# Four layers, four schedules: other norm heads, and values of two key heads padded apart

## The chip, the cores and the metric

The program runs on one core of a Trainium2 chip. The time is device time in microseconds (us), from one launch of the whole program; lower is better. Engines are TensorE (PE), VectorE (DVE), ScalarE (ACT), GpSimd (POOL) and SyncE (SP, which issues most DMAs).

## The reference: what is computed

One inference step of an encoder of four layers, on 256 prompt tokens and 64 sample tokens (320 together), width 1024, in float32. Layers 0 and 3 mix tokens by latent attention (MLA), layer 1 by stick-breaking attention (SB), layer 2 by sliding-window attention with 16 query heads over 4 key heads and a learned sink for each head (SWA; the "layer with sinks"). Each layer reads

```python
xp = xp + mp                    # mp = mixer(rms_norm(x))
xp = xp + fp                    # fp = conv_ffn(rms_norm(x)), inner width 2816
xp = xp + ple(xp, p_prompt[i], g_ple[i], w_ple_gate[i], w_ple_proj[i])
# ple = sigmoid(rms_norm(x, g) @ w_gate) * (p @ w_proj)
```

with the same for the sample tokens, which also read caches. In the layer with sinks

```python
m = jnp.maximum(jnp.max(s, axis=-1, keepdims=True), sink)
e = jnp.exp(s - m)
p = (e / (jnp.sum(e, axis=-1, keepdims=True) + jnp.exp(sink - m))).astype(v.dtype)
return jnp.einsum('bkgqs,bskd->bqkgd', p, v)
```

Outputs are the final norm of x and the new caches.

## The kernel before

**Layout.** Features lie on the 128 partitions, the 320 tokens on the free axis; x is eight tiles x0 to x7 of 128x320. A float32 product is made of three matmuls (`mm3`, L202 to L204): weight high part by data high part, high by low, low by high. So every operand exists as a pair: ScalarE writes the high part (L160), VectorE subtracts it from the source for the low part (L161); `split` does both.

**Weights.** They stream in 450 chunks of eight 128x128 tiles in the order of use (`fetch`, L168 to L176): SP loads `wraw` (three buffers), ScalarE makes `whi`, and VectorE or GpSimd makes `wlo`. GpSimd does so for every second chunk of the MLA and SB mixers and every third of SWA (`WPOOL`), while `self.wpool` is set; it is set at the mixer's start and cleared at its end. `more_weights` fetches ahead.

**Norms.** The gain is folded into the operand and the factor R = 1/rms is applied behind the projection, at its eviction. `norm_piece(m)` runs as soon as x tile m is final: `h{m}hi` (ScalarE, L305), `h{m}lo` (VectorE, L306), the square `sq` (ScalarE, L314), and the running sum `acc` (L320, on GpSimd but for the last). `norm_sums` sums columns on TensorE with a matrix of ones (L272) and takes the reciprocal root by Newton steps on VectorE (tiles `ncol`, L252 to L258). `spread` puts it on a diagonal (six VectorE operations on tiles called `sq`, L282 and L283), multiplies by minus ones on TensorE (L287), and ScalarE copies the result to `R` (L290).

**A layer.** Mixer; convolutional FFN; then `ple`, the per-layer embedding: its norm's sums and spread, then for each of eight columns a projection `pg`, a tanh, an update of x[m], and the next layer's `norm_piece(m)`. The operands of the FFN's and the embedding's norms are `h0` to `h7` and `ph0` to `ph7`. `prep` loads caches of the next layer and splits and transposes them; it is called ahead of `ple`. For SWA this is `swa_prep` (tiles `K00` to `K11` and `V0`, `V1`; the transposes use the PSUM tag "tp", which has two buffers and is also that of the column sums).

**SWA's core.** For two key-head tiles kt and two pairs of heads, `scores`, softmax (tiles `Pr`, `es`, `su`), `turn` (transposes of the probabilities, tiles `PT`) and `values` follow each other. A tile kt holds two key heads u side by side, 64 columns each. `values` makes, for each u, a PSUM tile with all 128 columns of V and splits only the 64 partitions of u:

```python
s = slice(64 * u, 64 * u + 64)
```

**Order.** A list scheduler with a cost model orders each engine's instructions from the program's order and priorities. Inside `manual_schedule(engines=...)` the named engines keep the program's order; before, that is TensorE alone at the mixers' heads.

## Time and the profile before

| | |
|---|---|
| runs, median of 3 | 1865.1 us (1860.9 to 1867.74) |
| the profiled execution | 1871.49 us, its span 1869.7 us |
| mean granted TensorE clock | 0.983 |
| busy share of the span | PE 96%, DVE 72%, ACT 52%, POOL 30% |
| DMA, mean | 136 GB/s |

The profiled execution is a little above the three runs. Stages by the trace, in us: MLA to 225, FFN 0 to 475, embedding 0 to 510, SB to 660, FFN 1 to 908, embedding 1 to 947, SWA to 1077, FFN 2 to 1320, embedding 2 to 1357, MLA to 1570, FFN 3 to 1820, embedding 3 and the final norm to the end. The granted clock has two levels here, 1.2 and 2.4 GHz (0.5 and 1.0 in the rows).

### The profile page before, as it was taken

The page shows a single profiled execution, that of the slowest core. Times are in us where ns is not written, and L with a number is a line of the kernel's source. Part 1 is how long each engine was busy: PE and PEld are TensorE (multiplying, and loading weights), DVE is VectorE, ACT ScalarE, POOL GpSimd, SP SyncE. Part 2 cuts the span into 40 slices and gives each one's busy share as a digit, 9 for nine tenths or more (in the row PEclk, how much of TensorE's full clock was granted, in tenths as well). Part 3 has the DMA queues.
Part 4 walks back from the last instruction along what each step waited for, and adds up shares of the span by engine and source line. Part 5 has one row for each costly group of instructions (what it writes and reads, how often), then busy time and mean ns, then how long its engine had stood idle before and what let it go on. Part 6 is the DMA issues. An engine that isn't in the chain of part 4 may idle for free.

```text
span 1869.7 us, 32633 instructions
## 1 busy us (share of the span) xinstructions
PE 1798.8 (96%) x12352; PEld 1775.2 (95%) x12352; DVE 1347.4 (72%) x2637; ACT 974.6 (52%) x1849; POOL 565.6 (30%) x834
## 2 busy tenths in 40 slices
PE   7899999999999999999998999999989999999996
PEld 7899999999999999999997899999988999999996
DVE  7876687754779878764578687764788777877546
ACT  5776644433568854433456654343447676434332
POOL 3433333321222234320145043320142334333103
PEclk9999999999999999999997999999999999999998
DMA  5333344444534344444342144444433333444441
GB/s 207 107 112 124 126 138 162 151 150 149 168 128 140 121 133 152 151 148 150 126 157 76 46 143 158 148 154 150 144 124 100 122 129 122 157 147 153 153 147 63
DMA packets 78126, 254.15 MB, mean 136 GB/s; under 512 B 9488, under 2 KB 18192, under 8 KB 77968
## 3 DMA queue, kind: packets, MB, share of 16 engines
q1 hardware_dynamic: 77248, 251.34, 40.5%
q8 instruction: 97, 1.59, 0.4%
q10 hardware_dynamic: 720, 0.71, 0.1%
q14 instruction: 61, 0.50, 0.1%
...
## 4 chain that ended last, share of the span: by engine, by line
PE 41%; DVE 6%; ACT 2%; issue 1%; POOL 1%; DMA 0%; DVEq 0%; SPq 0%; ACTq 0%; POOLq 0%
PE ps L202 13%; PE ps L203 13%; PE ps L204 13%; ACT whi L174 1%; DVE rsh L596 1%; DVE wlo L176 1%; PE ps L272 0%; PE ps L1188 0%; DVE PTl L161 0%; POOL wlo L176 0%; DVE h6lo L306 0%; DVE m L1165 0%; DMA ckt<-ckvT 0%; DVE m L671 0%; ACT Pr L675 0%
## 5 line engine op out<-in xcount | busy, mean ns | idle before, releaser
L174 ACT ACTIVATE whi<-wraw 128x1024 fp32r<-128x1024 f32 x450 | 474.5, 1056 | 443.0 <-PE ps L203 230.4
L176 DVE TENSOR_TENSOR wlo<-wraw,whi 128x1024 fp32r<-128x1024 f32 x381 | 471.1, 1237 | 226.5 <-ACT whi L174 219.5
L176 POOL TENSOR_TENSOR wlo<-wraw,whi 128x1024 fp32r<-128x1024 f32 x69 | 166.9, 2418 | 311.0 <-ACT whi L174 292.8
L384 POOL TENSOR_TENSOR ge<-cv,R 128x256 f32<-128x256 f32 (+1 forms) x176 | 132.8, 774 | 92.8 <-ACT cv L381 92.3
L320 POOL TENSOR_TENSOR acc<-acc,sq 128x320 f32<-128x320 f32 x72 | 77.4, 1075 | 261.6 <-ACT sq L314 259.0
L347 DVE TENSOR_TENSOR x<-x,ps 128x320 f32<-128x320 f32 x128 | 61.1, 482 | 55.7 <-PE ps L204 55.4
L379 DVE SCALAR_TENSOR_TENSOR cv<-G,cols,cv 128x322 f32<-128x322 f32 x176 | 95.9, 552 | 2.4
L388 DVE TENSOR_TENSOR af<-ge,ps 128x320 f32<-128x320 f32 x88 | 42.7, 486 | 67.6 <-POOL ge L384 67.4
L202 PE MATMUL ps<-h0hi,whi 128*128 128x320 f32 x256 | 81.1, 317 | 6.5 <-ACT h0hi L305 6.2
L203 PE MATMUL ps<-h6lo,whi 128*128 128x320 f32 x256 | 79.4, 310 | 3.3 <-DVE h6lo L306 3.3
L202 PE MATMUL ps<-h7hi,whi 128*128 128x320 f32 x256 | 79.2, 311 | 3.3 <-ACT h7hi L305 3.3
L203 PE MATMUL ps<-h0lo,whi 128*128 128x320 f32 x256 | 79.9, 312 | 0.8 <-DVE h0lo L306 0.8
L202 PE MATMUL ps<-h4hi,whi 128*128 128x320 f32 x256 | 79.6, 313 | 1.1 <-ACT h4hi L160 1.1
L203 PE MATMUL ps<-h5lo,whi 128*128 128x320 f32 x256 | 79.4, 310 | 1.2 <-DVE h5lo L161 1.2
L203 PE MATMUL ps<-h7lo,whi 128*128 128x320 f32 x256 | 79.9, 312 | 0.5 <-DVE h7lo L306 0.5
L202 PE MATMUL ps<-h1hi,whi 128*128 128x320 f32 x256 | 79.9, 312 | 0.0
L203 PE MATMUL ps<-h4lo,whi 128*128 128x320 f32 x256 | 79.7, 311 | 0.2 <-DVE h4lo L306 0.2
L203 PE MATMUL ps<-h3lo,whi 128*128 128x320 f32 x256 | 79.9, 312 | 0.0
L203 PE MATMUL ps<-h2lo,whi 128*128 128x320 f32 x256 | 79.9, 312 | 0.0
L203 PE MATMUL ps<-h1lo,whi 128*128 128x320 f32 x256 | 79.8, 312 | 0.0
L204 PE MATMUL ps<-h1hi,wlo 128*128 128x320 f32 x256 | 79.8, 312 | 0.0
L204 PE MATMUL ps<-h0hi,wlo 128*128 128x320 f32 x256 | 79.8, 312 | 0.0
...
## 6 DMA issues: line engine op xcount, KB each, us to landing
wraw<-w SPq DMA_DIRECT2D x450, 512.0 KB, 3.2
...
```

The lines of the kernel that those rows point to most:

```text
L174: nc.scalar.activation(out=hi, in_=raw, func=AF.Copy)
L176: e.tensor_tensor(out=lo, in0=raw, in1=hi.bitcast(F32), op=ALU.subtract)
L202: mm(out, w[0], x[0], start=first, stop=False, **kw)
L203: mm(out, w[0], x[1], start=False, stop=False, **kw)
L204: mm(out, w[1], x[0], start=False, stop=last, **kw)
L320: e.tensor_tensor(out=self.nacc[:, 0:NT], in0=self.nacc[:, 0:NT], in1=sq, op=ALU.add)
L347: self.nc.vector.tensor_tensor(out=self.x[m], in0=self.x[m], in1=p[:, 0:NT], op=ALU.add)
L379: nc.vector.scalar_tensor_tensor(out=cv, in0=gt[:, k:k + GW - 2], scalar=w[k], in1=cv, op0=ALU.mult, op1=ALU.add)
L384: nc.gpsimd.tensor_tensor(out=ge[:, c], in0=cv[:, c.start + o:c.stop + o], in1=R[:, c], op=ALU.mult)
L388: nc.vector.tensor_tensor(out=af, in0=ge, in1=pu[:, 0:NT], op=ALU.mult)
L596: nc.vector.tensor_tensor(out=lo[r, :].bitcast(F32R), in0=qf[r, :], in1=hi, op=ALU.subtract)
```

## The change

1. `norm_piece(7)` squares before it makes the operand; `acc` takes tile 6 on VectorE as well as tile 7.
2. The diagonal is made in `norm_sums` (`diag`), the matmul and R in `spread_mm`.
3. The SB mixer begins with `head`: projection A without its last row tile, then B, with the column sums behind B's second tile; then the last tiles of A and B; then the spread and C. From the last embedding column to the end of this head all four engines keep the program's order, and one chunk more is fetched ahead.
4. `self.wpool` is set by `headed`, behind a mixer's head. Chunks of the heads have their `wlo` on VectorE: VectorE makes 385 instead of 381, GpSimd 65 instead of 69.
5. In `ple` the next layer's `prep` comes behind the embedding's own norm.
6. SWA has no `prep`. Caches are loaded and split, and zeros written, in `keys` and `vals`. Its head is left to the list scheduler. V is padded apart: `V{kt}{u}` holds head u's 64 columns and zeros in the others, so that the products of both heads accumulate in one PSUM tile and three splits over 128 partitions stand for six over 64.
7. In the final norm `fin` carries the sign, and six outputs on VectorE read the spread from PSUM (`negR`); GpSimd does tiles 2 and 6 instead of 2 and 5.

```diff
     def norm_piece(self, m):
+        if m == NK - 1:
+            self.norm_square(m)
+            self.norm_operand(m)
+        else:
+            self.norm_operand(m)
+            self.norm_square(m)
...
-            e = nc.vector if m == NK - 1 or self.wpos == 0 else nc.gpsimd
+            e = nc.vector if m >= NK - 2 or self.wpos == 0 else nc.gpsimd
...
+    def head(self, A, B, C, keep_sum=False):
...
+        for k in range(NK - 1):
+            mm(0, k)
...
+        for k in range(NK - 1):
+            mm(1, k)
+            if k == 1:
+                self.norm_sums(keep_sum)
+        mm(0, NK - 1)
+        mm(1, NK - 1)
+        self.norm_spread()
+        self.proj(*C, h)
...
-            self.nr = self.newton_rsqrt(v)
+            self.nr = self.diag(self.newton_rsqrt(v))
...
         R = self.R
-        after()
+        prep = after()
...
+            if m == NK - 1 and nxt == 1:
+                self.region.enter_context(self.tc.manual_schedule(engines=ALL))
...
     def swa_prep(self, j, pool):
...
+        return None
...
+        self.headed(2)
+        h = self.norm_finish()
...
         def keys(kt):
-            kf, kh = KF[kt], K[kt]
+            kf = T([P, W], "kvf", bufs=2)
+            nc.sync.dma_start(out=kf[:, NT:W], in_=t["wkT"][kt])
...
+            kh = [pair([P, W], f"K{kt}{u}") for u in range(2)]
             for u in range(2):
+                for x in kh[u]:
+                    nc.gpsimd.memset(x[64 * (1 - u):64 * (2 - u), :].bitcast(F32), 0.0)
                 s = slice(64 * u, 64 * u + 64)
-                self.split(kh[u][0][s, 0:NT], kh[u][1][s, 0:NT], kf[s, 0:NT])
+                self.split(kh[u][0][s, :], kh[u][1][s, :], kf[s, :])
...
+            vh = [pair([P, 4, P], f"V{kt}{u}") for u in range(2)]
+            for u in range(2):
+                for x in vh[u]:
+                    nc.gpsimd.memset(x[:, :, 64 * (1 - u):64 * (2 - u)].bitcast(F32), 0.0)
+            pv = four(transposes([vf[:, c:c + P] for c in (0, P, S0 - 64, NT)]))
+            for u in range(2):
+                c = slice(64 * u, 64 * u + 64)
+                self.split(vh[u][0][:, :, c], vh[u][1][:, :, c], pv[:, :, c])
...
-            for u in range(2):
-
-                s = slice(64 * u, 64 * u + 64)
-                p, p2 = self.ps("tp"), self.ps("tp")
-                self.mm3(p[:, 0:256], vv(0), [flat(x[:, 4 + u]) for x in PT], True, True)
+            p, p2 = self.ps("tp"), self.ps("tp")
+            for u in range(2):
+                self.mm3(p[:, 0:256], vv(u, 0), [flat(x[:, 4 + u]) for x in PT], u == 0, u == 1)
...
+            for c, src in ((slice(0, P), p[:, 0:256]), (slice(P, SEQ), p[:, 256:512]), (slice(S0, NT), p2[:, 0:P])):
+                self.split(o[0][:, i2, c], o[1][:, i2, c], two(src))
...
+    def headed(self, kind):
+        self.region.close()
+        self.wpool = WPOOL[kind]
...
+            def after():
...
+                self.norm_start(f"g_mix{self.layers[n + 1]}")
+                return self.prep(self.layers[n + 1])
...
-            if m % 3 == 2:
-                nc.gpsimd.tensor_tensor(out=y, in0=self.fin[m], in1=self.R, op=ALU.mult)
+            if m % 4 == 2:
+                nc.gpsimd.tensor_tensor(out=y, in0=self.fin[m], in1=R, op=ALU.mult)
             else:
-                nc.vector.tensor_tensor(out=y, in0=self.fin[m], in1=self.R, op=ALU.mult)
+                nc.vector.tensor_tensor(out=y, in0=self.fin[m], in1=self.negR, op=ALU.mult)
```

**TensorE at the head of SB, before.** `ps_6362` is the first projection of the mixer, here its last two row tiles; `ps_6393` is the second, whose 24 matmuls stand ahead of the column sums.

```order
L202 MATMUL ps_6362<-h6hi_6306,whi_6273 128x320
L203 MATMUL ps_6362<-h6lo_6307,whi_6273 128x320
L204 MATMUL ps_6362<-h6hi_6306,wlo_6274 128x320
L202 MATMUL ps_6362<-h7hi_6349,whi_6273 128x320
L203 MATMUL ps_6362<-h7lo_6350,whi_6273 128x320
L204 MATMUL ps_6362<-h7hi_6349,wlo_6274 128x320
L202 MATMUL ps_6393<-h0hi_6006,whi_6316 128x320
L203 MATMUL ps_6393<-h0lo_6007,whi_6316 128x320
```

The same place in the change: `ps_6368` is A, `ps_6369` is B, `ps_6404` the column sums.

```order
L205 MATMUL ps_6368<-h6hi_6306,whi_6273 128x320
L206 MATMUL ps_6368<-h6lo_6307,whi_6273 128x320
L207 MATMUL ps_6368<-h6hi_6306,wlo_6274 128x320
L205 MATMUL ps_6369<-h0hi_6006,whi_6318 128x320
L206 MATMUL ps_6369<-h0lo_6007,whi_6318 128x320
L207 MATMUL ps_6369<-h0hi_6006,wlo_6319 128x320
L205 MATMUL ps_6369<-h1hi_6057,whi_6318 128x320
L206 MATMUL ps_6369<-h1lo_6058,whi_6318 128x320
L207 MATMUL ps_6369<-h1hi_6057,wlo_6319 128x320
L275 MATMUL ps_6404<-ones_112,acc_6012 128x2 x3
L205 MATMUL ps_6369<-h2hi_6113,whi_6318 128x320
```

The last row tile of the first projection went from 21 rows behind that projection's start to 43, and the column sums from 48 rows to 27.

**VectorE at the same head, before.** G is the embedding's gate, x_14 and x_15 are x tiles 6 and 7, `ncol` the first Newton tile.

```order
L429 TENSOR_TENSOR G_1286_6344<-ps_6313,R_5941 128x320
L306 SCALAR_TENSOR_TENSOR h6lo_6307<-x_14_99,gains_73,h6hi_6306 128x320
L431 SCALAR_TENSOR_TENSOR G_1286_6344<-G_1286_6344,ps_6220 128x320
L433 TENSOR_TENSOR x_15_101<-x_15_101,G_1286_6344 128x320
L306 SCALAR_TENSOR_TENSOR h7lo_6350<-x_15_101,gains_73,h7hi_6349 128x320
L320 TENSOR_TENSOR acc_6012<-acc_6012,sq_6353 128x320
L176 TENSOR_TENSOR wlo_6454<-wraw_6451,whi_6453 128x1024
L335 TENSOR_SCALAR ncol_6428<-ps_6424 128x3
```

In the change:

```order
L486 TENSOR_TENSOR G_1289_6352<-ps_6315,R_5906 128x320
L325 SCALAR_TENSOR_TENSOR h6lo_6307<-x_14_99,gains_73,h6hi_6306 128x320
L344 TENSOR_TENSOR acc_6012<-acc_6012,sq_6310 128x320
L488 SCALAR_TENSOR_TENSOR G_1289_6352<-G_1289_6352,ps_6220 128x320
L490 TENSOR_TENSOR x_15_101<-x_15_101,G_1289_6352 128x320
L344 TENSOR_TENSOR acc_6012<-acc_6012,sq_6357 128x320
L325 SCALAR_TENSOR_TENSOR h7lo_6361<-x_15_101,gains_73,h7hi_6360 128x320
L179 TENSOR_TENSOR wlo_6395<-wraw_6392,whi_6394 128x1024
L387 TENSOR_SCALAR ncol_6408<-ps_6404 128x3
```

`acc` of tile 6 stands on VectorE, `acc` of tile 7 ahead of `h7lo`, and the chunk whose `wlo` GpSimd made in the head (not seen in the first list) is the `wlo_6395` of the second.

**VectorE ahead of embedding 1's Newton steps, before.** ph7 is the last operand of that norm; K and V are SWA's cache parts from `swa_prep`, and the transposes that V0l and V1l read hold both "tp" buffers.

```order
L306 SCALAR_TENSOR_TENSOR ph7lo_11114<-x_15_101,gains_73,ph7hi_11113 128x320
L320 TENSOR_TENSOR acc_10479<-acc_10479,sq_11117 128x320
L161 TENSOR_TENSOR K00l_11135<-kf_2161_11124,K00h_11134 64x128
L161 TENSOR_TENSOR K01l_11137<-kf_2161_11124,K01h_11136 64x128
L161 TENSOR_TENSOR K10l_11153<-kf_2163_11128,K10h_11152 64x128
L161 TENSOR_TENSOR K11l_11155<-kf_2163_11128,K11h_11154 64x128
L176 TENSOR_TENSOR wlo_11291<-wraw_11288,whi_11290 128x1024
L161 TENSOR_TENSOR V0l_11147<-ps_11148,V0h_11146 128x128
L161 TENSOR_TENSOR V1l_11165<-ps_11166,V1h_11164 128x128
L335 TENSOR_SCALAR ncol_11174<-ps_11170 128x3
```

In the change:

```order
L179 TENSOR_TENSOR wlo_11203<-wraw_11200,whi_11202 128x1024
L344 TENSOR_TENSOR acc_10482<-acc_10482,sq_11116 128x320
L325 SCALAR_TENSOR_TENSOR ph7lo_11120<-x_15_101,gains_73,ph7hi_11119 128x320
L179 TENSOR_TENSOR wlo_11248<-wraw_11245,whi_11247 128x1024
L387 TENSOR_SCALAR ncol_11128<-ps_11124 128x3
```

The six cache splits left this place.

**VectorE in one call of `values`, before** (a stretch of it; u = 0 writes ps_12117 and ps_12118, u = 1 ps_12140 and ps_12141).

```order
L161 TENSOR_TENSOR O0l_12116<-ps_12117,O0h_12115 64x2x128
L1167 TENSOR_SCALAR nb_12514<-m_12513 128x2
L1168 TENSOR_TENSOR es_12515<-cols_111,m_12513 128x2
L161 TENSOR_TENSOR O0l_12116<-ps_12140,O0h_12115 64x2x128
L1215 MEMSET ps_12529 64x4x64
L1165 TENSOR_REDUCE m_12543<-ps_12529 128x4
L161 TENSOR_TENSOR O0l_12116<-ps_12140,O0h_12115 64x2x128
L161 TENSOR_TENSOR O0l_12116<-ps_12141,O0h_12115 64x2x64
```

The whole call in the change:

```order
L164 TENSOR_TENSOR O0l_12105<-ps_12106,O0h_12104 128x2x128
L1220 TENSOR_SCALAR Pr_12239<-Pr_12239,su_12238 128x192
L1244 MEMSET ps_12465 64x2x64
L164 TENSOR_TENSOR O0l_12105<-ps_12107,O0h_12104 128x2x64
L1245 MEMSET ps_12465 64x2x64
L164 TENSOR_TENSOR O0l_12105<-ps_12106,O0h_12104 128x2x128
```

Six splits of 64 partitions became three of 128, and one pair of PSUM tiles serves both heads.

## Rows read from the trace of the kernel before

**Rows 1.** The page: the span, its busy times, and the chain that ended last.

```profile
span 1869.7 us, 32633 instructions
...
PE 1798.8 (96%) x12352; PEld 1775.2 (95%) x12352; DVE 1347.4 (72%) x2637; ACT 974.6 (52%) x1849; POOL 565.6 (30%) x834
...
PE 41%; DVE 6%; ACT 2%; issue 1%; POOL 1%; DMA 0%; DVEq 0%; SPq 0%; ACTq 0%; POOLq 0%
```

**Rows 2.** Windows of 20 us: length, busy time (instructions) by engine, granted clock, DMA share, GB/s.

```profile
480.00:500.00 20.00, 18.84 (x127) 18.34 (x126) 17.40 (x37) 11.87 (x21) 3.51 (x4) 1.00 0.40 132
500.00:520.00 20.00, 17.62 (x107) 16.87 (x107) 14.11 (x19) 8.82 (x14) 5.91 (x6) 0.91 0.46 152
...
900.00:920.00 20.00, 17.75 (x105) 17.36 (x104) 10.22 (x30) 5.56 (x11) 2.09 (x5) 0.85 0.44 139
...
940.00:960.00 20.00, 17.63 (x118) 16.88 (x118) 15.49 (x23) 9.33 (x15) 4.79 (x4) 1.00 0.49 159
...
980.00:1000.00 20.00, 16.23 (x115) 15.57 (x114) 15.53 (x48) 13.21 (x38) 14.85 (x16) 0.98 0.33 113
1000.00:1020.00 20.00, 15.90 (x92) 15.02 (x91) 19.20 (x63) 14.55 (x49) 11.12 (x14) 0.76 0.24 80
1020.00:1040.00 20.00, 17.82 (x106) 16.97 (x106) 13.16 (x51) 11.42 (x42) 0.85 (x2) 0.75 0.00 0
1040.00:1060.00 20.00, 19.64 (x128) 19.39 (x129) 13.21 (x42) 13.12 (x41) 0.35 (x2) 0.83 0.16 55
...
1320.00:1340.00 20.00, 18.77 (x120) 18.52 (x119) 14.11 (x38) 8.76 (x18) 1.37 (x2) 0.91 0.30 99
...
1360.00:1380.00 20.00, 17.81 (x121) 17.33 (x122) 15.17 (x36) 7.41 (x12) 6.81 (x6) 1.00 0.33 110
...
260.00:280.00 20.00, 20.00 (x139) 20.00 (x138) 17.63 (x34) 11.06 (x17) 10.26 (x26) 1.00 0.41 134
```

**Rows 3.** TensorE's waits by releaser: total us, how often, the longest.

```profile
PE ps L287 <- DVE sq L282: 4.5, 3, 2.9
...
PE ps L202 <- ACT Pr L1173: 3.4, 3, 1.9
...
PE ps L202 <- ACT h7hi L305: 3.3, 3, 1.1
PE ps L203 <- DVE h6lo L306: 3.3, 3, 1.1
...
PE ps L272 <- DVE Vl L161: 2.4, 2, 1.2
...
PE ps L272 <- DVE V0l L161: 2.3, 1, 2.3
```

**Rows 4.** Timeline of GpSimd, then VectorE, ahead of the stick-breaking layer.

```profile
509.72 2.39 POOL L176 TENSOR_TENSOR wlo<-wraw,whi 128x1024 fp32r<-128x1024 f32 x1 [1.61 <-ACT whi L174]
...
510.12 2.33 DVE L306 SCALAR_TENSOR_TENSOR h6lo<-x,gains,h6hi 128x320 fp32r<-128x320 f32 x1 [0.33 <-ACT h6hi L305]
...
514.16 0.55 DVE L306 SCALAR_TENSOR_TENSOR h7lo<-x,gains,h7hi 128x320 fp32r<-128x320 f32 x1 [0.63 <-ACT h7hi L305]
```

**Rows 5.** Timeline of VectorE, then TensorE, at layer 1's embedding norm.

```profile
907.92 0.49 DVE L320 TENSOR_TENSOR acc<-acc,sq 128x320 f32<-128x320 f32 x1
...
914.00 1.44 PE L272 MATMUL ps<-ones,acc 128*128 128x2 f32 x6 [2.25 <-DVE V0l L161]
```

**Rows 6.** O0l by shape, ns min/median/max; from the timeline a key split, a clear.

```profile
L161 DVE TENSOR_TENSOR O0l<-ps,O0h x16: 208/398/429, 562.9 to 1043.6; 64x256 fp32r<-64x256 f32 x10, 64x128 fp32r<-64x128 f32 x4, 64x64 fp32r<-64x64 f32 x2
...
974.63 1.06 DVE L161 TENSOR_TENSOR K01l<-kf,K01h 64x320 fp32r<-64x320 f32 x1
...
898.52 0.47 POOL L1077 MEMSET K00h<- 64x448 f32 x1
```

**Rows 7.** Timeline of the last operations: ScalarE, then VectorE.

```profile
1861.97 0.44 ACT L290 ACTIVATE R<-ps 128x320 f32<-128x320 f32 x1 [6.45 <-PE ps L287]
...
1862.85 1.15 DVE L1341 TENSOR_TENSOR h1hi<-h1lo,R 128x320 f32<-128x320 f32 x1
```

More of the change, by code (lines that the diff above doesn't have):

```diff
@@ L276, in spread, with diag @@
     def spread(self, r, pool, tag, bufs=2):
+        return self.spread_mm(self.diag(r), pool, tag, bufs)
+    def diag(self, r):
         nc = self.nc
@@ L284, in spread, with spread_mm @@
                                            op0=ALU.mult, op1=ALU.subtract)
+        return dg
+    def spread_mm(self, dg, pool, tag, bufs=2, sign=-1.0):
+        nc = self.nc
         p = self.ps("tp")
@@ L289, in spread @@
         rb = self.tile(pool, [P, NT], tag, bufs=bufs)
[L290 removed]
+        self.negR = p[:, 0:NT]
+        nc.scalar.activation(out=rb, in_=p[:, 0:NT], func=AF.Copy, scale=sign)
         return rb
@@ L328, in norm_finish @@
         return self.nh
+    def head(self, A, B, C, keep_sum=False):
+        h = self.nh
+        if self.first:
+            w = [[self.take(name, np.arange(k * P, k * P + P), cols) for k in range(NK)] for _, name, cols in (A, B, C)]
+            for k in range(NK):
+                for x, y in zip((A, B, C), w):
+                    self.mm3(x[0], y[k], h[k], k == 0, k == NK - 1)
+            self.norm_sums(keep_sum)
+            return
+        first = [(p, [self.take(name, np.arange(k * P, k * P + P), cols) for k in range(NK)]) for p, name, cols in (A,)]
+        mm = lambda n, k: self.mm3(first[n][0], first[n][1][k], h[k], k == 0, k == NK - 1)
+        for k in range(NK - 1):
+            mm(0, k)
+        p, name, cols = B
+        first.append((p, [self.take(name, np.arange(k * P, k * P + P), cols) for k in range(NK)]))
+        for k in range(NK - 1):
+            mm(1, k)
+            if k == 1:
+                self.norm_sums(keep_sum)
+        mm(0, NK - 1)
+        mm(1, NK - 1)
+        self.norm_spread()
+        self.proj(*C, h)
     def norm_sums(self, keep_sum=False):
@@ L404, in ffn, with ple @@
         return ph, pl
-    def ple(self, i, pool, p_emb, after):
+    def ple(self, i, pool, p_emb, after, nxt):
         nc = self.nc
@@ L427, in ple @@
             self.proj(pg[:, 0:NT], f"pg{i}", cols, h)
+            if m == NK - 1 and nxt == 1:
+                self.more_weights()
             u = self.tile(pool, [P, NT], "G2", bufs=2)
@@ L434, in ple @@
             self.norm_piece(m)
+        return prep
     def rotate(self, pool, src, out, o=DEC):
@@ L901, in project, with weighed @@
                 st[r] = start(r)
-            bd, KT, V = st[r]
-            p = self.ps(tag)
-            self.proj(p[:, 0:NT], f"sq{j}", n * D + np.arange(r * P, r * P + P), h)
+            p, *w = weighed(r, n, tag)
+            self.proj(p, *w, h)
             return lambda: scaled(r, n, p)
+        def weighed(r, n, tag="mm"):
+            return self.ps(tag)[:, 0:NT], f"sq{j}", n * D + np.arange(r * P, r * P + P)
         def scaled(r, n, p):
@@ L1012, in values @@
             O.append(o)
+        ps = [weighed(0, n) for n in range(3)]
+        self.head(*ps)
+        self.headed(1)
         with self.tc.manual_schedule(engines=PE):
-            pq, pk = project(0, 0), project(0, 1)
-            self.norm_sums()
-            pv = project(0, 2)
+            with self.tc.high_priority(AHEAD):
+                scaled(0, 0, ps[0][0])
+                scaled(0, 1, ps[1][0])
             pq1 = project(1, 0, "sc")
-            self.norm_spread()
+            scaled(0, 2, ps[2][0])
             pk1 = project(1, 1, "sc")
-            with self.tc.high_priority(AHEAD):
-                pq()
-                pk()
-            pv()
         self.tc.keep_in_program_order(nc.scalar.preload_act_table_set("natural_log_exp_and_others"))
@@ L1090, in swa, with project @@
         W = NT + WIN
+        self.load_rot(pool)
         T = lambda shape, tag, dt=F32, bufs=1: self.tile(pool, shape, tag, dt, bufs)
         pair = lambda shape, tag, bufs=1: self.pair(pool, shape, tag, bufs)
-        h = self.nh
-        early = {}
-        def product(m, tag="mm"):
-            p = self.ps(tag)
-            self.proj(p[:, 0:NT], f"wq{j}", swa_cols(m), h)
-            return p
-        with self.tc.manual_schedule(engines=PE):
-            for n, m in enumerate((8, 10, 0, 1, 2, 3)):
-                early[m] = product(m, "mm" if n < 3 else "sc")
-                if n == 1:
-                    self.norm_sums()
-                if n == 3:
-                    self.norm_spread()
-        def project(m):
-            p = early.pop(m) if m in early else product(m)
+        self.headed(2)
+        h = self.norm_finish()
+        R = self.R
+        tags = ["sc"] * 3 + ["mm"] * 3
+        def project(m):
+            p = self.ps(tags.pop() if tags else "mm")
+            self.proj(p[:, 0:NT], f"wq{j}", swa_cols(m), h)
             f = T([P, NT], "pf", bufs=2)
-            nc.vector.tensor_tensor(out=f, in0=p[:, 0:NT], in1=self.R, op=ALU.mult)
+            nc.vector.tensor_tensor(out=f, in0=p[:, 0:NT], in1=R, op=ALU.mult)
             return f
@@ L1146, in vals @@
             nc.sync.dma_start(out=t["o_wv"][kt], in_=vf)
-            pv = transposes([vf[:, c:c + P] for c in (0, P, S0 - 64)])[:, 0:3 * P]
-            self.split(vh[0][:, 0:3], vh[1][:, 0:3], pv.rearrange("p (a b) -> p a b", a=3))
+            vh = [pair([P, 4, P], f"V{kt}{u}") for u in range(2)]
[6 more added lines that the diff above has]
+                self.split(vh[u][0][:, :, c], vh[u][1][:, :, c], pv[:, :, c])
+            V.append(vh)
         st = {}
```

70 lines of the change are left out of this document (25 added, 45 removed).

## The prediction

> **What bounds the kernel now.** I read the page first: TensorE is busy for 96% of a span of 1869.7 us, and it has 41% of the chain that ended last, the other engines together some 9% [rows 1]. So time can only be won where TensorE stands or runs at its lower clock. The windows say where. A full window of 20 us has 139 matmuls at clock 1.00, so one 128x320 matmul is issued every 0.144 us [rows 2]. For any other window I count as lost its idle time (20 less the busy time) and (1 - clock) x 20. This gives 1.2 us for 480 to 500, 2.4 + 1.8 for 500 to 520 (head of SB), 2.25 + 3.0 for 900 to 920 (embedding 1), 2.4 + 0 for 940 to 960 (head of SWA), 1.2 + 1.8 for 1320 to 1340 (embedding 2) and 2.2 + 0 for 1360 to 1380 (head of the last MLA). In SWA's core, 980 to 1060, four windows give idle 3.8 + 4.1 + 2.2 + 0.4 = 10.4 and clock 0.4 + 4.8 + 5.0 + 3.4 = 13.6, together 24 us. That is the largest single place, and in its second window VectorE is busy for 19.2 of 20 us.
>
> The waits name what ends the idle time: the operands h6lo and h7hi, three times each 1.1 us; V0l and Vl ahead of the column sums, 2.3 and 2.4; the diagonal ahead of the spread, 4.5, of which 2.9 is one wait at the very end; the softmax tile Pr, 3.4 [rows 3].
>
> Why h6lo is late is seen in one place of the timeline: GpSimd's `wlo` runs from 509.72 for 2.39 us, and VectorE's h6lo, begun at 510.12, takes 2.33; the same operation at 514.16 takes 0.55 [rows 4]. An operation that shares time with GpSimd's `wlo` thus loses 1.8 us.
>
> **The change, part by part.** The sum is made against the profiled execution, 1871.5 us, which stands 6.4 above the median of the runs; what I win there I take off the median.
>
> Head of SB. No GpSimd `wlo` is left in it, so h6lo takes 0.55 and TensorE's first 1.1 us wait is gone. The second operand pair, h7, moves 22 matmuls back (3.2 us), and with it the second wait goes. New is an early wait at the column sums: behind h6lo (ready near 510.7) VectorE has acc of tile 6, G and x, 0.49 us each by the like operation of [rows 5], then ScalarE's square and acc of tile 7, together near 513.2. TensorE would be there nine matmuls after its h6lo, which was at about 511.4: 512.7. So 0.5 us stay of 2.4. The spread stands 46 rows behind the sums, 6.6 us, and the Newton steps and the diagonal need less. Of the 1.8 us of clock I take 1.6. Gain 3.5; without the clock 1.9, and with a wait of 1.4 at the sums, 1.0; at most 4.2.
>
> Embedding 1. `acc` ends at 908.4, yet the column sums start at 914.00, 2.25 us idle, waiting for V0l, as the transposes behind V0l and V1l hold the two buffers that the sums need [rows 5]. With `prep` gone from there the sums have no one ahead of them. Gain 5.0 of 5.2 with the clock; 2.2 without.
>
> Embedding 2. The same with Vl: the transposes move behind the sums. Gain 2.4 of 3.0; 1.2 without the clock. Embedding 0: the diagonal stands earlier; 0.7 of 1.2, or nothing.
>
> Head of the last MLA. Chunks 330 and 332 leave GpSimd, so h6lo's 1.1 us go; h7hi stands behind its square now, about 0.5 later, so that wait stays, perhaps longer. One `wlo` in the Newton steps moves too. Gain 1.5, between 0 and 2.2. The first head moves one chunk: one collision is 1.8 at most, taken as 0.5.
>
> End. Six outputs don't wait for ScalarE's copy, 0.44 us, and two of them that take 1.15 beside GpSimd [rows 7] should take 0.5, as they then read PSUM: 0.44 + 2 x 0.65 = 1.75. Taken as 1.5, at least 0.5.
>
> SWA. Removed: in four calls of `values`, six splits of 64 partitions become three of 128, at 0.40 us for 64x256 [rows 6], and some 0.28 for the smaller, by the least and the middle of that row. That is 4 x (4 x 0.40 + 2 x 0.28) / 2 = 4.3 us on VectorE and nearly as much on ScalarE, in the stretch where VectorE is full. One pair of PSUM tiles instead of two takes a wait out of each call. TensorE's matmuls are the same thirty. Added: the cache's K and V are split inside the layer. K's splits grow from 64x320 to 64x448; one took 1.06 beside GpSimd [rows 6], so 4 x 0.2 to 4 x 0.4. V has four splits where there were two large and two small: about 0.5. Together 1.3 to 2; net 3 us less on VectorE. The first scores stand 24 matmuls later in the order, 3.5 us, and the head's 2.4 us of waits come off, since other projections' early tiles stand ahead of h6 and h7: about 1 later. GpSimd gets sixteen clears of zeros ahead of the rotary work, some 7 us at 0.47 for one [rows 6]; before, eight of them lay in the FFN. I set 3 for VectorE, 4.5 for a third of the 13.6 us of clock, and minus 1 for the late start: 6.5, taken as 6. The bounds are wide, as no row shows this order. Upward: two thirds of the clock, VectorE's 3 and the head's 2.4, some 15. Downward: no relief, half of the clears on the path (3.5) and the late start, minus 5. I stay nearer the middle since VectorE bounds only one of the four windows.
>
> Taken at nothing: the twelve `acc` additions that go to VectorE (0.49 each). At the FFN and embedding heads a whole projection's matmuls cover them; without that cover it would be 12 x 0.5 = 6 us. The extra SP loads are a small share of 136 GB/s.
>
> Sum: 0.5 + 0.7 + 3.5 + 5.0 + 6 + 2.4 + 1.5 + 1.5 = 21. 1871.5 - 21 = 1850.5; off the median, **1844 us**.
>
> **The clock, weighed.** The same pair of waits lowered the clock at the head of SB (0.91) and not at the head of SWA (1.00) [rows 2]; so a drop does not follow from the gaps alone, and closing them need not return it. The Trainium skill, "TensorE: Matmul & The Clock Gate", Part 1, says that the activity watch behind the clock runs free of the program, so that the same kernel's slow stretches vary between executions; this trace, with its two like heads, agrees. By it half of the clock terms (1.6 + 2.8 + 1.2 + 4.5 = 10.1) might be no gain of the change, and the sum would be 16.
>
> **Rivals.** I call faster what is below the median by over 0.5% (under 1855.8), slower what is above 1874.4: about what measuring this kernel can tell from no change.
>
> *SWA opens up.* With VectorE eased the chain of scores, softmax, transposes and values closes up and the clock stays whole: 15 instead of 6, total 30, 1835. For it: the full VectorE window and the half-clock that follows it. Against: in 1020 to 1040 VectorE is busy for 13 us only and TensorE still loses 7. 0.15, and 0.03 for still more.
>
> *The clock doesn't come back.* Idle gaps close, the lower stretches fall elsewhere: 21 - 10 = 11, 1854. For it: the two like heads above. 0.20.
>
> *The gaps only move.* The lists show new order, not new slack: h7hi behind its square, acc on a busy VectorE, and what SWA's core gains it gives back at its head. Then embedding 0 gives 0.3, SB 1, embedding 1 its 2.2, embedding 2 its 1.2, the end 1.5: 6, 1859. 0.12.
>
> *The second half of SWA starves.* The caches now pass through `kvf`, two buffers for four tiles, and the loads for kt = 1 queue on SP behind the stores of kt = 0's results. If they come late, the keys of kt = 1, their split, the scores and all behind stand, and TensorE idles with nothing of FFN 2 to fill in. Elsewhere I have 15 us of gain, so it decides from 15 + 9.4 = 24 us lost in SWA, which would double that core's present loss: 1875 to 1885. Against: TensorE has whole projections of other tiles to do before kt = 1 is due. 0.05.
>
> **How the numbers follow.** Forecast 1838 to 1851: 0.45. With the rivals 1826 to 1838 (0.15), 1850 to 1857 (0.20), 1857 to 1861 (0.12), 1875 and more (0.05), below 1826 (0.03). The range 1827 to 1860 leaves out 0.05 + 0.03 and the edges of two cases. Faster is 0.45 + 0.15 + 0.03 and 0.13 of the clock's 0.20, 0.76; same the rest of it and the moved gaps, 0.19; slower 0.05.
>
> **What would show it.** Right: no TensorE wait for V0l or Vl ahead of sums and 139 matmuls in the windows of embeddings 1 and 2; h6lo at 0.55 us at the head of SB and under 1 us idle there; the outputs at the end at 0.5 us each; SWA's core, to the start of FFN 2, shorter by some 6 us. Wrong: SWA's stage as long as before or longer, with waits for K or V tiles or a GpSimd busy with clears; clock below 1 in the windows whose gaps closed; new waits at the column sums, of 1 us or more, for acc.

## The result, and the profile after

The changed kernel took 1851.56 us (median of 6 runs, 1849.81 to 1853.82), the kernel before 1866.12 (6 runs, 1860.4 to 1867.74) beside it: a ratio of 0.9923, 95% interval 0.9906 to 0.9939, or 14.6 us less. The forecast was 1844, with 1827 to 1860 as its range. The profiled execution took 1852.02 us with a span of 1850.2: 19.5 us under the span of [rows 1].

The page after: the span, busy times by engine, the chain that ended last.

```profile
span 1850.2 us, 32625 instructions
...
PE 1786.0 (97%) x12352; PEld 1763.4 (95%) x12352; DVE 1344.3 (73%) x2637; ACT 969.2 (52%) x1833; POOL 541.1 (29%) x826
...
PE 83%; DVE 9%; ACT 5%; issue 2%; POOL 1%; DMA 1%; SPq 0%; DVEq 0%; ACTq 0%; POOLq 0%
```

TensorE is busy for 12.8 us less, though it has the same number of instructions; the mean granted clock is 0.989, where it was 0.983. Its shares of the last chain, 41% before and 83% now, can't be compared: those of [rows 1] add up to some 51%, as that chain is followed back only to 912 us. Of what was followed, TensorE has four fifths in both.

Windows of 20 us after (length, busy time and instructions by engine, clock, DMA share, GB/s):

```profile
500.00:520.00 20.00, 19.47 (x135) 19.23 (x134) 15.86 (x36) 7.85 (x13) 1.71 (x4) 1.00 0.40 132
560.00:580.00 20.00, 19.14 (x133) 18.28 (x132) 16.33 (x30) 17.26 (x40) 4.21 (x3) 1.00 0.38 125
580.00:600.00 20.00, 19.33 (x135) 18.58 (x134) 17.97 (x36) 18.14 (x45) 3.42 (x4) 1.00 0.43 136
620.00:640.00 20.00, 18.88 (x128) 17.79 (x127) 17.87 (x33) 13.43 (x33) 5.08 (x3) 1.00 0.35 115
900.00:920.00 20.00, 20.00 (x140) 20.00 (x139) 11.75 (x29) 6.26 (x10) 0.00 (x0) 1.00 0.38 122
940.00:960.00 20.00, 20.00 (x140) 20.00 (x139) 16.71 (x31) 8.15 (x13) 11.41 (x19) 1.00 0.56 177
980.00:1000.00 20.00, 15.05 (x109) 14.21 (x107) 18.41 (x54) 14.75 (x42) 13.46 (x16) 0.98 0.33 106
1000.00:1020.00 20.00, 15.21 (x95) 14.99 (x95) 17.55 (x65) 12.39 (x49) 7.26 (x9) 0.68 0.10 35
1020.00:1040.00 20.00, 18.80 (x149) 18.20 (x148) 18.03 (x63) 17.21 (x62) 0.41 (x2) 1.00 0.08 28
1040.00:1060.00 20.00, 20.00 (x154) 20.00 (x153) 11.32 (x24) 9.75 (x20) 3.58 (x3) 1.00 0.24 80
1300.00:1320.00 20.00, 19.24 (x133) 18.73 (x132) 15.31 (x40) 10.10 (x19) 1.32 (x2) 1.00 0.42 140
1340.00:1360.00 20.00, 17.66 (x109) 16.91 (x108) 12.27 (x32) 6.75 (x11) 1.91 (x1) 0.91 0.33 109
```

The head of SB (500 to 520) is at clock 1.00 with 0.5 us idle, where [rows 2] had 4.2 us lost; embedding 1 (900 to 920) is full, where 5.2 were lost, and so is SWA's head (940 to 960), where 2.4 were. New idle time stands in SB's core, 560 to 640. SWA's core begins some 5 us earlier here: its worst window is still 1000 to 1020, idle 4.8 us and clock 0.68, but from 1020 to 1060 nothing is at the lower clock, where [rows 2] had 0.75 and 0.83. The last MLA's head (now in 1340 to 1360) lost 2.3 us of idle and 1.8 of clock; before it lost 2.2 and nothing. The first window of embedding 2 (1300 to 1320) loses 0.8, where [rows 2] had 1.2 of idle and 1.8 of clock at that place.

TensorE's waits after (total us, how often, the longest):

```profile
PE ps L1227 <- DVE PTl L164: 8.0, 3, 6.0
...
PE ps L275 <- DVE acc L344: 3.8, 2, 3.3
PE ps L297 <- DVE sq L288: 3.8, 3, 2.9
...
PE ps L205 <- ACT Pr L1212: 2.4, 1, 2.4
...
PE ps L205 <- DVE A2l L164: 1.3, 2, 0.7
PE ps L205 <- ACT h7hi L324: 1.3, 1, 1.3
...
PE ps L275 <- DVE Vl L164: 1.2, 1, 1.2
...
PE ps L205 <- DVE su L1024: 0.9, 2, 0.5
PE ps L206 <- DVE h6lo L325: 0.9, 1, 0.9
```

V0l is gone from this list, and one of the two waits for Vl, that of embedding 2; the other stands in layer 0, near 19 us, in both kernels, and was never the change's to win. For h6lo and h7hi TensorE waits once each, not three times [rows 3]. The wait for the diagonal at the end is still 2.9. One wait is new and long: transposes of the probabilities in SWA stand 6.0 us for PTl.

**Where the 19.5 us came from.** FFNs take the same 235.0 us in every trace, from their first matmul on h0hi to the embedding's first on ph0hi. Between them I measured from the embedding's first matmul to the next FFN's first, for each profiled execution (layer 0 from the first matmul of all, some 6 us into the span); kernels below the second line are the experiments that follow. The medians are of all runs, the stages of one execution each.

| kernel | median us | layer 0 | emb. 0 + SB | emb. 1 + SWA | emb. 2 + MLA | emb. 3 + end |
|---|---|---|---|---|---|---|
| before | 1866.1 | 231.1 | 199.5 | 177.1 | 264.2 | 51.5 |
| the change | 1851.6 | 231.2 | 200.2 | 158.6 | 263.9 | 50.0 |
| old_values | 1859.8 | 229.8 | 200.7 | 170.2 | 262.2 | 50.3 |
| pad_alone | 1857.7 | 232.5 | 198.9 | 167.6 | 265.2 | 50.9 |
| ple_order | 1859.7 | 230.4 | 199.0 | 166.1 | 263.1 | 50.9 |
| sb_head_old | 1850.4 | 232.0 | 200.1 | 158.7 | 264.2 | 50.6 |
| two_parts | 1854.5 | 233.2 | 197.4 | 159.8 | 263.9 | 51.2 |
| split64 | 1864.5 | 233.7 | 199.8 | 168.9 | 265.2 | 50.9 |
| swa_no_gp | 1851.4 | 232.1 | 200.0 | 157.5 | 263.6 | 49.9 |
| mla_late | 1848.8 | 232.3 | 201.2 | 158.0 | 258.4 | 49.9 |
| after_again | 1850.7 | 230.3 | 200.3 | 158.6 | 262.8 | 50.0 |
| best | 1846.6 | 232.6 | 200.6 | 155.7 | 259.1 | 49.9 |
| three_edits | 1849.3 | 230.3 | 198.7 | 159.8 | 259.0 | 50.9 |

Of the 19.5 us, 18.5 come from embedding 1 with SWA. Layer 0 shows the noise: in pad_alone, ple_order, two_parts and split64 it has the code of the kernel before, and takes 230.4 to 233.7. Embedding 0 with SB has a pattern: 197.4 to 199.8 in the six executions with the old code of SB, 200.0 to 201.2 in the six with the new head, and 200.1 in sb_head_old.

### The profile page after: what moved, and what is told of

Read it like the earlier page. It is cut to its first block, busy times and chain, and to the rows that moved or that the text cites. A ratio compares the mean times of both kernels' runs of the same rounds, so it can differ in the third digit from the quotient of the medians.

```text
span 1850.2 us, 32625 instructions
## 1 busy us (share of the span) xinstructions
PE 1786.0 (97%) x12352; PEld 1763.4 (95%) x12352; DVE 1344.3 (73%) x2637; ACT 969.2 (52%) x1833; POOL 541.1 (29%) x826
## 4 chain that ended last, share of the span: by engine, by line
PE 83%; DVE 9%; ACT 5%; issue 2%; POOL 1%; DMA 1%; SPq 0%; DVEq 0%; ACTq 0%; POOLq 0%
PE ps L205 27%; PE ps L206 26%; PE ps L207 26%; ACT whi L177 2%; DVE wlo L179 1%; DVE rsh L654 1%; PE ps L753 1%; PE ps L275 0%; DVE ncol L261 0%; DMA wraw<-w 0%; ACT Pr L733 0%; PE ps L700 0%; PE ps L701 0%; PE ps L1227 0%; DVE KR L541 0%
## 5 line engine op out<-in xcount | busy, mean ns | idle before, releaser
L179 DVE TENSOR_TENSOR wlo<-wraw,whi 128x1024 fp32r<-128x1024 f32 x385 | 476.6, 1239 | 224.5 <-ACT whi L177 217.5
L179 POOL TENSOR_TENSOR wlo<-wraw,whi 128x1024 fp32r<-128x1024 f32 x65 | 157.2, 2419 | 317.8 <-ACT whi L177 294.0
L436 POOL TENSOR_TENSOR ge<-cv,R 128x256 f32<-128x256 f32 (+1 forms) x176 | 138.2, 805 | 88.5 <-ACT cv L433 88.1
L344 POOL TENSOR_TENSOR acc<-acc,sq 128x320 f32<-128x320 f32 x60 | 61.0, 1017 | 226.3 <-ACT sq L338 225.1
L207 PE MATMUL ps<-h7hi,wlo 128*128 128x320 f32 x256 | 79.7, 312 | 0.0
L205 PE MATMUL ps<-h2hi,whi 128*128 128x320 f32 x256 | 79.7, 311 | 0.0
```

The lines of the kernel that those rows point to most:

```text
L179: e.tensor_tensor(out=lo, in0=raw, in1=hi.bitcast(F32), op=ALU.subtract)
L205: mm(out, w[0], x[0], start=first, stop=False, **kw)
L207: mm(out, w[1], x[0], start=False, stop=last, **kw)
L344: e.tensor_tensor(out=self.nacc[:, 0:NT], in0=self.nacc[:, 0:NT], in1=sq, op=ALU.add)
L436: nc.gpsimd.tensor_tensor(out=ge[:, c], in0=cv[:, c.start + o:c.stop + o], in1=R[:, c], op=ALU.mult)
```

## The experiments

**old_values.** The change without padded V. The diff, cut to its core:

```diff
-            vh = [pair([P, 4, P], f"V{kt}{u}") for u in range(2)]
...
+            vh = pair([P, 4, P], f"V{kt}")
+            self.split(vh[0], vh[1], four(transposes([vf[:, c:c + P] for c in (0, P, S0 - 64, NT)])))
...
+            for u in range(2):
+                s = slice(64 * u, 64 * u + 64)
+                p, p2 = self.ps("tp"), self.ps("tp")
...
+                    self.split(o[0][s, i2, c], o[1][s, i2, c], two(src)[s])
```

> The changed kernel with V in one pair of tiles and the values of the two key heads in two rounds, as before; all else of the change stays. The layer with sinks went from 136.8 to 124.2 us. Theory (the merged splits are what eased it): about 8 of these 12.6 us come back, that layer takes 132 and the kernel some 1859. Rival (the layer gains by its head's order and by caches taken inside): under 2.5 us come back, 1851 to 1854.

Measured: 1859.76 us (10 runs; ratio to before 0.9968, 0.9955 to 0.9982), and 11.6 us longer than the change in the stage of SWA; the layer alone takes 135.8, not 132. Its windows:

```profile
1000.00:1020.00 20.00, 13.22 (x72) 12.51 (x73) 17.09 (x61) 11.93 (x45) 6.62 (x8) 0.69 0.08 27
1020.00:1040.00 20.00, 17.81 (x108) 16.94 (x107) 12.36 (x48) 12.45 (x45) 0.21 (x1) 0.76 0.00 1
1040.00:1060.00 20.00, 19.66 (x144) 19.41 (x143) 14.89 (x39) 14.35 (x39) 2.60 (x2) 0.95 0.24 80
```

Against the change, 1020 to 1040 falls from 149 matmuls at clock 1.00 to 108 at 0.76. By the medians the padded V and its merged values carry 8 of the 14.6 us.

**pad_alone.** The kernel before with that part alone:

```diff
-            vh = pair([P, 4, P], f"V{kt}")
+            vh = [pair([P, 4, P], f"V{kt}{u}") for u in range(2)]
...
+                self.split(vh[u][0][:, 0:3, c], vh[u][1][:, 0:3, c], pv[:, :, c])
...
+            p, p2 = self.ps("tp"), self.ps("tp")
+            for u in range(2):
+                self.mm3(p[:, 0:256], vv(u, 0), [flat(x[:, 4 + u]) for x in PT], u == 0, u == 1)
```

> The kernel before with the padded V and merged values alone. Theory (merged splits): the layer with sinks shortens by 6 to 9 us, the kernel to about 1858 to 1860, with nothing changed in other layers. Rival (order of the head): shorter by under 2.5 us, the kernel at 1863 to 1867.

Measured: 1857.68 us (10 runs; 0.9963, 0.9947 to 0.998), 8.2 below the 1865.89 of the kernel before beside it. The layer with sinks takes 127.3 in the profiled execution, the slowest of the ten. Its windows:

```profile
1000.00:1020.00 20.00, 16.10 (x94) 15.51 (x93) 19.31 (x63) 14.95 (x50) 10.90 (x13) 0.76 0.24 80
1020.00:1040.00 20.00, 19.49 (x133) 19.14 (x133) 13.39 (x56) 11.37 (x45) 1.11 (x2) 0.81 0.00 1
1040.00:1060.00 20.00, 20.00 (x156) 19.96 (x156) 15.92 (x42) 14.58 (x42) 2.59 (x2) 1.00 0.24 81
```

Its splits into O0l of 256 columns between 900 and 1100 us (busy us, mean ns), and those of the kernel before:

```profile
L161 DVE TENSOR_TENSOR O0l<-ps,O0h 128x256 fp32r<-128x256 f32 x4 | 1.6, 405 | 0.0
...
L161 DVE TENSOR_TENSOR O0l<-ps,O0h 64x256 fp32r<-64x256 f32 x8 | 3.3, 414 | 2.0 <-ACT O0h L160 1.8
```

In the same order of work as before, 1000 to 1020 stays as it was [rows 2], and the gain begins where the values are made: 0.5 us idle instead of 2.2 in 1020 to 1040, and 1040 to 1060 at full clock. A split of 128x256 takes what one of 64x256 took, 405 ns against 414, and there are half as many.

**split64.** pad_alone, but each result split in two halves (the diff is against pad_alone):

```diff
-                self.split(o[0][:, i2, c], o[1][:, i2, c], two(src))
+                for s in (slice(0, 64), slice(64, P)):
+                    self.split(o[0][s, i2, c], o[1][s, i2, c], two(src)[s])
```

> The kernel before with padded V and merged values, but each of the three results split as two halves of 64 partitions: 24 operations each on ScalarE and VectorE again, one pair of PSUM tiles for a call as in the change. Theory (the time on VectorE and ScalarE that the splits take is what was saved): the gain of the padded V alone, 8 us, goes, to 1864 to 1867. Rival (one round on the two PSUM tiles instead of two is what helps): it stays, 1857 to 1860.

Measured: 1864.51 us (10 runs; 0.9994, 0.9982 to 1.0006). That is 6.8 above pad_alone, with the same matmuls; the theory held.

```profile
900.00:920.00 20.00, 18.94 (x131) 18.57 (x130) 11.54 (x33) 7.15 (x15) 6.74 (x17) 1.00 0.49 166
1000.00:1020.00 20.00, 16.10 (x104) 15.51 (x103) 19.09 (x62) 14.87 (x50) 11.47 (x14) 0.83 0.23 80
1020.00:1040.00 20.00, 14.74 (x106) 13.74 (x104) 15.66 (x60) 12.46 (x46) 0.51 (x2) 0.91 0.00 0
1040.00:1060.00 20.00, 19.85 (x140) 19.78 (x141) 15.14 (x42) 15.39 (x45) 2.36 (x2) 0.91 0.17 55
```

1020 to 1060 loses again 5.3 us idle in its first half and clock in both. So it is the time of twelve splits on ScalarE and twelve on VectorE that was saved; one round on the PSUM tiles instead of two gives next to nothing by itself (1.2 us between the medians, and the ratio's interval holds 1). The first row I keep for the clock, below.

**ple_order.** The kernel before with the cache preparation behind the embedding's norm:

```diff
         R = self.R
-        after()
+        prep = after()
...
-                prep = self.prep(self.layers[n + 1])
-                self.ple(i, ple, e, lambda: self.norm_start(f"g_mix{self.layers[n + 1]}"))
+                def after():
+                    self.norm_start(f"g_mix{self.layers[n + 1]}")
+                    return self.prep(self.layers[n + 1])
+                prep = self.ple(i, ple, e, after)
```

> The kernel before with one edit: the next layer's cache preparation behind the embedding's own norm. Theory: TensorE's waits for V0l and Vl ahead of the column sums go, 2.3 and 1.2 us, with the half-clock stretches behind them; embedding 1 shortens by 4 to 5 us, embedding 2 by 2, the kernel to about 1859. Rival: the cache work only moves into the mixer's head, where h6lo and h7hi wait on the same VectorE, and the sum of embedding and mixer stays within 2 us.

Measured: 1859.74 us (9 runs, 1857.51 to 1866.77; 0.998, 0.9961 to 0.9999). Its window of embedding 1:

```profile
900.00:920.00 20.00, 20.00 (x139) 19.84 (x139) 12.75 (x35) 7.92 (x15) 1.55 (x4) 1.00 0.50 160
```

Full, with no wait ahead of the column sums there: embedding 1 alone is 5.5 us shorter. Embedding 2 with the MLA is 1.1 shorter, not 2. In this execution SWA was 5.5 shorter as well (131.3), though its core has the old code: over the layer it idles as long as before (13.9 us, 13.8), but loses 6.8 us to the clock instead of 13.7. The runs spread over 9 us, so the ratio's interval nearly reaches 1. Five of them, at a mean granted clock of 0.987 to 0.989, took 1857.5 to 1859.7, the other four, at 0.982 to 0.985, 1862.9 to 1866.8.

**sb_head_old.** The change with the head of SB as before (the regions of four engines and the split order gone, and the evictions behind the head in their old order):

```diff
-        ps = [weighed(0, n) for n in range(3)]
-        self.head(*ps)
-        self.headed(1)
         with self.tc.manual_schedule(engines=PE):
+            pq, pk = project(0, 0), project(0, 1)
+            self.norm_sums()
+            pv = project(0, 2)
...
```

> The changed kernel with the stick-breaking layer's head as before (TensorE alone in program order, GpSimd's weight parts from the mixer's start). In the change that head is 4 us shorter and the layer's body 5 us longer. Theory (the body is paced by its chain over VectorE and ScalarE, so a shorter head is given back): the layer takes 162 to 164 us as before, and the kernel is not slower than the change, 1849 to 1852. Rival (the body's loss has another cause, such as the order that the scheduler chose for it, and the head's gain is real): the kernel is 4 us slower, about 1855.5.

Measured: 1850.40 us (4 runs; 0.9924, 0.99 to 0.9948). Its windows:

```profile
500.00:520.00 20.00, 17.13 (x98) 16.31 (x97) 14.72 (x20) 8.93 (x14) 4.51 (x5) 0.84 0.43 144
560.00:580.00 20.00, 20.00 (x139) 19.54 (x139) 19.35 (x39) 17.81 (x42) 4.45 (x3) 1.00 0.41 136
580.00:600.00 20.00, 20.00 (x139) 19.49 (x139) 17.67 (x34) 16.73 (x40) 4.98 (x3) 1.00 0.42 136
620.00:640.00 20.00, 20.00 (x140) 19.44 (x140) 18.21 (x39) 16.93 (x41) 5.54 (x3) 1.00 0.29 100
```

Its head loses 2.9 us idle and 3.2 of clock, and then 560 to 640 has 139 and 140 matmuls with nothing idle. The change has the full head, and in the same three windows it idles 0.9 + 0.7 + 1.1 us with 133, 135 and 128 matmuls. Both stages take 200 us, and the medians are 1.2 us apart: the head's gain is given back. The layer alone takes 165.1, where 162 to 164 was expected.

**two_parts.** pad_alone and ple_order together, by the same lines.

> The kernel before with two edits: padded V with merged values, and the cache preparation behind the embedding's norm. Alone they gave 8 and 6 us by medians, the whole change 14. Theory (these two are the whole of it; the new heads, the weight parts moved to VectorE and the end give nothing that stays): 1851 to 1853. Rival (they overlap, since both act on the layer with sinks, and the rest of the change gives some 4 us): 1855 to 1858.

Measured: 1854.45 us (7 runs; 0.9945, 0.9928 to 0.9963): 11.2 of the change's 14.6. Neither number was met; it lies between the two, and three us are left for all other parts. One window of its SWA core, and that of SB's head, which has its old code:

```profile
1000.00:1020.00 20.00, 15.70 (x109) 14.67 (x109) 19.07 (x65) 12.91 (x46) 9.01 (x11) 0.91 0.16 54
...
500.00:520.00 20.00, 17.63 (x118) 16.88 (x117) 14.89 (x19) 10.08 (x18) 5.90 (x6) 1.00 0.43 139
```

**swa_no_gp.**

```diff
-WPOOL = (2, 2, 3)
+WPOOL = (2, 2, 0)
```

> The changed kernel, in the layer with sinks all low parts of weights on VectorE, none on GpSimd. Theory (GpSimd's parts of 2.4 us stretch small operations of the softmax on VectorE, one of them to 1.7 us, and these stand in the chain that TensorE waits for): the layer gets 1 to 4 us shorter, 1848 to 1850. Rival (VectorE is full there, and six or seven more operations of 1.24 us lengthen it): 2 to 6 us longer, 1853 to 1857.

Measured: 1851.37 us (4 runs; 0.993, 0.991 to 0.995), level with the change, so neither held; the stage of SWA is 1.1 us shorter in the one execution that shows it. What GpSimd's part does is seen in the change's timeline (GpSimd, then VectorE):

```profile
1000.12 2.34 POOL L179 TENSOR_TENSOR wlo<-wraw,whi 128x1024 fp32r<-128x1024 f32 x1
...
1000.77 1.72 DVE L1206 TENSOR_SCALAR nb<-m 128x2 f32<-128x2 f32 x1
```

An operation of 128x2, some 0.16 us in quiet stretches, took 1.72. That doing without these stretches is worth about as much as the extra operations on VectorE cost (1.24 us each) would explain the level times; it was not separated.

**mla_late.** The change with two edits:

```diff
-            dkv(0)
-            dkv(1)
+            b0, b1 = dkv_begin(0), dkv_begin(1)
+            dkv(0, b0)
+            dkv(1, b1)
...
         self.negR = p[:, 0:NT]
+        if early:
+            early()
```

`dkv_begin` does row tiles 0 to 5 of a projection, and `dkv` now only tiles 6 and 7; `early` issues output 1 ahead of the copy to R.

> The changed kernel with two further edits, at places far apart. In the MLA head the last two row tiles of the first two projections stand behind the other six of both. Theory: the waits for h6lo and h7hi in the last layer, 0.9 and 1.3 us, go, and its stage of 231 us is 2 us shorter. Rival (given back in the core behind it, as in the stick-breaking layer): the stage stays within 1 us. At the end, the first output on VectorE is issued ahead of ScalarE's copy of the spread; if that copy is what VectorE waits for, the first output starts 0.4 us sooner behind the spread's matmul; if not, nothing moves. Together 1849 against 1851.6.

Measured: 1848.84 us (4 runs; 0.9918, 0.9897 to 0.9939). The last layer with its embedding is 5.5 us shorter; layer 0 runs the same MLA code and shows no gain (232.3). The head of the last layer:

```profile
1340.00:1360.00 20.00, 19.75 (x135) 19.18 (x134) 15.41 (x48) 9.46 (x17) 2.76 (x3) 1.00 0.45 144
```

135 matmuls against 109 in the change, at full clock. The end, in the order spread, first output, copy, next output:

```profile
1837.72 1.35 PE L297 MATMUL ps<-sq,negones 128*128 128x320 f32 x2 [2.90 <-DVE sq L288]
...
1839.11 0.49 DVE L1396 TENSOR_TENSOR h1hi<-h1lo,ps 128x320 f32<-128x320 f32 x1 [0.73 <-PE ps L297]
...
1839.63 0.44 ACT L303 ACTIVATE R<-ps 128x320 f32<-128x320 f32 x1 [6.29 <-DVE h1hi L1396]
...
1840.10 0.49 DVE L1396 TENSOR_TENSOR h0hi<-h0lo,ps 128x320 f32<-128x320 f32 x1 [0.50 <-ACT R L303]
```

The first output starts 1.39 us behind the spread's matmul instead of 1.85, as it no longer waits for the copy; but then the copy waits for it, and the other outputs for the copy. The end takes as long as in the change.

**after_again, best, three_edits** ran side by side. best is swa_no_gp with the late row tiles of mla_late; three_edits is two_parts with them.

> The changed kernel once more, as the measure for the two kernels run beside it on the same chip. Both theories: 1850 to 1853.

> The changed kernel with the last two row tiles of the MLA head's first two projections behind the other six, and no GpSimd weight parts in the layer with sinks. Theory (the waits for h6lo and h7hi, 2.2 us, were on the path of the last layer and are not given back): 1847 to 1849.5, at least 2 us below the changed kernel of this same call. Rival (the 2.7 us between the medians of two calls came from the chip or the clock): within 1 us of the changed kernel.

> The kernel before with three edits: padded V and merged values, cache preparation behind the embedding's norm, and the late row tiles in the MLA head. Theory (these three carry nearly all; the head of the stick-breaking layer, the weight parts and the end are worth 3 us at most): 1851 to 1852.5, level with the changed kernel. Rival (the late tiles help only where h6lo is not stretched beside GpSimd, which still happens in this version): no better than the 1854.5 of the two edits.

Measured: after_again 1850.70 us (6 runs, 1849.04 to 1853.4; 0.9924, 0.9907 to 0.9941), best 1846.56 (5 runs, 1844.9 to 1849.14; 0.9902, 0.9883 to 0.992), three_edits 1849.29 (6 runs, 1846.78 to 1855.65; 0.9921, 0.9901 to 0.9942). best is the fastest, 4.1 us under the change on the same chip by the medians, though the intervals of the ratios overlap. three_edits is level with the whole change and 5.2 under two_parts, which lacks only the late row tiles. best and three_edits came out faster than their theories had it (1847 to 1849.5, 1851 to 1852.5); their rivals are out.

## Why the prediction came out as it did

The direction, the range and the two largest places were right; the sum of 21 met the 19.5 between the two profiled executions, and missed the 14.6 between the medians. That it met the 19.5 is luck: SWA gave 6.6 more than its term, the head of SB 4.2 less, embedding 2 with the last MLA's head 3.6 less. The median, 1851.56, lies 7.6 above the 1844 forecast, inside the range, but in the band that was given to *The clock doesn't come back*. That rival's mechanism is not what happened, as the clock did come back: its mean in the change's six runs is 0.987 to 0.990. The step that made 1844 too low is taking off the median what was counted on one slower execution (see the base, below).

**SWA, 6 us: the mechanism right, the size too small.** The layer alone went from 136.8 to 124.2, by 12.6. The 4.3 us of saved splits on VectorE were counted rightly: in this layer they take 9.0 us before and 4.5 after (ScalarE's half 8.2 and 4.4). Alone, the padded V gives 8.2 us, and split64 takes nearly all of it away. In 980 to 1060 pad_alone loses, by the same count as in [rows 2], 3.8 + 3.9 + 0.5 + 0 idle (its first window, not shown, is busy for 16.24 at clock 1.00) and 4.8 + 3.8 of clock, 16.8 against 24: 2.2 us of idle time and 5.0 of clock. So the mis-sized term is the clock, of which I took a third; over the whole layer the change loses 6.8 us to it, where before 13.7 were lost. By this pair of executions the rival that SWA opens up, with 15, was nearer than my 6. But the 12.6 leans on the execution before: ple_order, with the old values, lost 6.8 us to the clock as well, and against its 131.3 the change gains 7.1. The other parts in this layer nearly cancel. two_parts, with the caches prepared ahead and the old head, has 159.8 for the stage, the change 158.6: the head's waits are gone, but TensorE then stands 6.0 us for PTl in the core, and 1000 to 1020 is at clock 0.68, not 0.91. Whether that is the late start of which I took off 1 us was not tried.

**Embedding 1, 5.0: right against this execution.** Its stage went from 40.3 to 34.4, and ple_order alone brought 34.8. But split64, which keeps the old order there, took 36.1, as its clock did not fall, and pad_alone, which keeps it too, 40.3. So against split64 1.7 of the 5.9 us are left, and the rest comes only where the clock would have fallen.

**Head of SB, 3.5: wrong.** The step itself is in the profile as I told it. h6lo takes 0.55, and half a us stays at the column sums, of 3.8 in the list (the other 3.3 is the end's). What failed is that I let the gain stand without asking what the core behind it could take. With the old head TensorE is full through that core, with the new one it idles for A2l, su and others, the products of VectorE's and ScalarE's chain. It is "the gaps only move" for this layer: the sum for its stage is +0.7 us, and sb_head_old is no slower. That the chain is what the core waits for is seen in the waits. It is not the whole cause: with the old code and no clock lost at the head (1.00 in 500 to 520), two_parts takes 197.4 for this stage, 2.6 us or more under every kernel with the new head. A core that only waited for a chain of fixed length would not get longer. What in the new order adds to it was not tried.

**Embedding 2 and the last MLA's head, 2.4 + 1.5: 0.3 in the profiled execution.** The column sums of embedding 2 lost their wait for Vl and the clock behind it, some 2.2 us by the windows above; but the head kept its idle time and now lost 1.8 of clock, so the two nearly cancel. The VectorE timeline of the change, first at SB's head, then at this one:

```profile
509.34 0.55 DVE L325 SCALAR_TENSOR_TENSOR h6lo<-x,gains,h6hi 128x320 fp32r<-128x320 f32 x1 [0.23 <-ACT h6hi L324]
...
1339.17 1.21 DVE L179 TENSOR_TENSOR wlo<-wraw,whi 128x1024 fp32r<-128x1024 f32 x1
...
1340.70 0.54 DVE L325 SCALAR_TENSOR_TENSOR h6lo<-x,gains,h6hi 128x320 fp32r<-128x320 f32 x1
```

At this head GpSimd's part is gone, and h6lo takes 0.54; but the chunk's low part now runs on VectorE ahead of it, 1.21 us in the same queue, with one operation of 0.47 between. I priced what leaves GpSimd and not what then stands in line on VectorE. With h7hi behind its square TensorE waited 0.9 and 1.3 us, and the clock fell. mla_late, where these two tiles are needed later, shows that this head is on the path: 5.5 us of the stage, 2.7 to 4.1 between medians (with swa_no_gp's edit in the larger). Unlike SB's, this gain is not given back.

**The end, 1.5: size nearly right, route half wrong.** Against the execution before it is 1.5; five others with the old end took 50.9 to 51.2, which leaves about 1. The profile shows the spread, the copy, and two outputs:

```profile
1841.88 1.35 PE L297 MATMUL ps<-sq,negones 128*128 128x320 f32 x2 [2.90 <-DVE sq L288]
...
1843.27 0.44 ACT L301 ACTIVATE R<-ps 128x320 f32<-128x320 f32 x1 [5.77 <-PE ps L297]
...
1843.73 0.49 DVE L1386 TENSOR_TENSOR h0hi<-h0lo,ps 128x320 f32<-128x320 f32 x1 [1.19 <-ACT R L301]
...
1844.14 0.48 DVE L1386 TENSOR_TENSOR h1hi<-h1lo,ps 128x320 f32<-128x320 f32 x1
```

The outputs read PSUM and take 0.48 instead of the 1.15 of [rows 7], as said. They still start behind ScalarE's copy: the releaser named is that copy, and in mla_late, with the two in the other order, the copy waits for the output. So in this program the second reader of the PSUM tile waits for the first, and the 0.44 us did not come.

**Layer 0 and embedding 0, 0.5 and 0.7:** nothing that stands out of the noise, and 0.7 (36.1 to 35.4). That 0.7 isn't the change's either: pad_alone and split64, with the old code there, took 35.4 and 35.2.

**The base.** The profiled execution before, 1871.5, is above every timed run of that kernel beside the experiments (51 runs, 1859.4 to 1869.4), while that of the change, 1852.0, lies among its own. Some five us of the 21 belong to that one execution, which lies 5.4 above the median of 1866.1. The clock is a part of it. Embedding 1 lost 3.0 us to the clock in [rows 2]; split64 has all but the same preparation ahead of the same sums, and its first row above shows 900 to 920 at clock 1.00. The 51 runs show the same: 15 with a mean granted clock of 0.987 to 0.989 took 1859.4 to 1864.4 us (median 1861.1), 26 with 0.982 to 0.984 took 1865.9 to 1869.4. The twelve runs of the change, its own six and after_again's, all have 0.987 or more, with a median of 1851.1. So at a like clock the change is worth some 10 us, by the same count padded V 5.6 and ple_order 2.8, near its 2.25 us of idle time; the rest of each gain between medians is that the lower clock came less often. This is an estimate from few runs. The Trainium skill, "TensorE: Matmul & The Clock Gate", Part 1, has it that the number of matmuls at the lower clock, when a kernel starts, varies between runs of one kernel. The runs above agree that it varies, here in mid-kernel: the profiles of like code in layer 0 spread over 3 us.
